# Low parts of the down weights by an accumulating transfer on GpSimd's queue, instead of VectorE's difference

## Chip, cores and metric

One core of a Trainium2 chip. The metric is the device time of one execution in microseconds. The kernel before took 1913.95 us (median of 3 runs, 1913.91 to 1914.23).

## What is computed

A decoder trunk of two layers on 512 tokens with 1024 features, all in float32. Each layer is a feed-forward block, a mixer and a second feed-forward block; the mixer is a gated linear attention (GLA) in layer 0 and a stick-breaking attention (SB) in layer 1. There are therefore four feed-forward blocks. Cut to what matters here:

```python
def swiglu(h, w_gate, w_up, w_down):
    return (jax.nn.silu(h @ w_gate) * (h @ w_up)) @ w_down

for i in range(DEPTH):
    x = x + 0.5 * swiglu(rmsnorm(x, ffn1_norm[i]), ffn1_w_gate[i], ffn1_w_up[i], ffn1_w_down[i])
    ...                                   # the mixer
    x = x + 0.5 * swiglu(rmsnorm(x, ffn2_norm[i]), ffn2_w_gate[i], ffn2_w_up[i], ffn2_w_down[i])
return rmsnorm(x, final_norm)
```

`w_gate` and `w_up` are 1024 x 2816, `w_down` is 2816 x 1024.

## The kernel before

**Numbers in two parts.** TensorE multiplies in fp32r, a shortened float32. To keep the precision, each operand v is split into a high part, v rounded to fp32r, and a low part, v minus the high part. A product is then three matmuls: high x high, low x high, high x low (`mm3`, L62 to L65). In the trace `wh` and `wl` are the high and low parts of weights; `hh` and `hl` (`nh`, `nl`, `xh`, `xl`, `th`, `tl`) are those of activations.

**The weight stream.** All weights pass through `Chunk`, `Entry` and `Feed` in the order of use. `Chunk.load` (L77) issues the load on SyncE's (SP's) queue, L85. Chunks of the down weights carry `few = True` and go to the tile `rawd`, which has two buffers of 512 KB; other chunks go to `raw`, two buffers of 1 MB. `Entry.split` (L94) makes the two parts of each unit of 128 x 1024 elements: ScalarE casts the raw unit into `wh` (L103), and VectorE subtracts, `wl = raw - wh` (L105). `wh` and `wl` have four buffers each, shared by all kinds of units. `Feed.start` splits up to two entries ahead of the one that is multiplied, and loads up to five ahead.

**The feed-forward block.** The 2816 inner features go in chunks of 256, the chunks in groups (`GROUPS`). Gate and up of a group are multiplied, and between them the down products of the group before. A down unit (`down`, L261) is 24 matmuls of 128 x 512 into the bank `ps_d`; VectorE then adds half of the bank to the residual (L276). A block has 22 down units, and the last block 18, since its last group goes through `back_tok`; that makes 84. From chunk 3 on the gate's products, and from chunk 2 on those of up, go by seven products of half size (L487, banks `ps_w`, `ps_z`, `ps_q`). VectorE then makes sums of the raw weights (tile `s`), which are split like weights. In this steady stage one gate or up chunk by seven products and one down unit take turns. ScalarE copies the first product out of `ps_w` (L522) and of `ps_q` (L530) before a second product is added to the same bank. Where a group ends, several down units follow each other, at the end of a block four or five.

**What sets the order.** The program is written in the order of the entries, and a scheduler then places the instructions of each engine's queue; each engine runs its queue in order and waits on semaphores. Transfers of one queue are issued in order. GpSimd's queue holds little: a few constants, the small gate weights of the GLA mixer (L703 to L722) and one load for the final norm (L1144).

Of the kernel before, what the change touches and what calls it, by code (L numbers as in the profile page):

```python
# [18 lines left out]
P = 128  # L19
T = 512  # L20
# [10 lines left out]
def decoder(ctx: ExitStack, tc: tile.TileContext, a: dict, out: bass.AP):  # L31
    nc = tc.nc

    # ---------------------------------------------------------------- pools
# [16 lines left out]
    # ------------------------------------------------------------ constants  # L51
# [15 lines left out]
    # --------------------------------------------------------- weight stream  # L67
    # Every weight matrix passes through here in the order of use: chunks of 1 MB are
    # loaded, cut into units of 4 KB a partition, split into high and low parts, and
    # multiplied. An entry is one or more units with the products that use them.  # L70
# [17 lines left out]
    class Entry:  # L88
        """units: (chunk, view of it, n, m); body(W) yields between parts of the products."""
# [4 lines left out]
        def split(self):  # L94
            if self.W is None:
                self.W = []
                for ch, view, n, m in self.units:
                    r = view(ch.load())
                    few = n * m < 1024
                    pool, x, bufs = (st["few"], "v", 1) if few else (wp, "w", 4)  # L100
                    h = pool.tile([P, n, m], F32R, tag=x + "h", bufs=bufs, name="wh")
                    l = pool.tile([P, n, m], F32R, tag=x + "l", bufs=bufs, name="wl")
                    st["cut"] = nc.scalar.copy(h, r).ins  # L103
                    with tc.issue_after(st["gains"]):
                        nc.vector.tensor_tensor(out=l, in0=r, in1=h.bitcast(F32), op=ALU.subtract)  # L105
                    self.W.append((h, l))
# [46 lines left out]
    def feat(ch, f, evac, tag=None, defer=None):  # L153
        """features f*128.. of a [P, KD, 256] chunk on partitions, all tokens"""

        def body(W):
            (wh, wl), = W
            ps = psum("ps_f", tag)
            for part in (range(0, KD // 2), range(KD // 2, KD)):
                for k in part:  # L160
                    mm3(ps, wh[:, k], wl[:, k], st["h"][k], st["l"][k], k == 0, k == KD - 1)
                if part[-1] == KD - 1:
                    if defer is None:
                        evac(ps)
                    else:
                        defer.append((evac, ps))
                yield

        feed.q.append(Entry([(ch, lambda t: t[:, :, f * P : (f + 1) * P], KD, P)], body))

    def tok(w, c0, evac, tag=None):
        """columns c0..c0+256 with the tokens on partitions; evac(i, ps[P, 256])"""
        ch = Chunk(cols(w, c0, 256), KD, 256)

        def body(W):
            ps = None
            for i in range(NT):
                if i % 2 == 0:
                    ps = psum("ps_t", tag)
                o = ps[:, (i % 2) * 256 : (i % 2) * 256 + 256]  # L180
                s = slice(i * P, (i + 1) * P)
                for k in range(KD):
                    wh, wl = W[k // 4]
                    mm(o, st["h"][k][:, s], wh[:, k % 4], k == 0, False)
                    mm(o, st["h"][k][:, s], wl[:, k % 4], False, False)
                    mm(o, st["l"][k][:, s], wh[:, k % 4], False, k == KD - 1)
                if i % 2:
                    evac(i - 1, ps[:, 0:256])
                    evac(i, o)
                yield  # L190

        feed.q.append(
            Entry([(ch, (lambda t, u=u: t[:, u * 4 : u * 4 + 4]), 4, 256) for u in range(2)], body)
        )

    def back(w, r0, nf, hs, scale, nxt, late=0, tags=(None,) * 8):
        """x[d] += scale * sum_f w[r0 + f, d] h[f]; nxt(k) runs when x[k] is done.
        The last `late` blocks of h come late: their products wait for the end."""
# [62 lines left out]
    def down(w, r0, nf, hs, part, nxt):  # L261
        """x[d] += 0.5 * sum_f w[r0 + f, d] h[f] for the 8 / nf blocks d of a part"""
# [22 lines left out]
    def back_tok(w, r0, nf, hs, done):  # L285
        """the same with tokens on partitions: done(dh, i, ps) gets 512 features of token tile i"""
# [23 lines left out]
    # ----------------------------------------------------------------- norms  # L310
# [24 lines left out]
    def stats_a(tag=None):  # L335
        """r4[token, tile]: 1 / rms of the residual"""
        if st["ss"] is None:
            sums = st["sums"]
        else:
            ps = psum("ps_st", tag)  # L340
            for i in range(NT):
                mm(ps[:, i : i + 1], st["ss"][:, i * P : (i + 1) * P], ones[:, 0:1], True, True)
            sums = ps[:, 0:NT]
        st["r4"] = rstd(sums, NT)
# [15 lines left out]
    def stats_b(tag=None):  # L360
        """R[any partition, token]: the same along the free axis"""
# [11 lines left out]
    def two_halves(between=None):  # L373
        """the next two entries, the first half of both before the second"""
        feed.finish()
        g = [feed.start(), feed.start()]
        for i in range(3):
            for x in g:
                next(x, None)
            if i == 0 and between is not None:  # L380
                between()
# [13 lines left out]
    def act(o, i, fn, **kw):  # L395
        """an activation of the Exp and Ln tables, queued behind their load"""
        with tc.issue_after(st["tab"]):
            st["last"] = nc.scalar.activation(o, i, fn, **kw).ins

    # ------------------------------------------------------------------- FFN  # L400
    class FFN:
        """The chunks of 256 features go in groups: gate and up, with down for the group
        before between them. From product NORMED on the input is scaled by 1/rms ahead of
        it. The gate's products from chunk SEVEN on, and those of up for the chunks SEVEN_UP,
        go by Winograd's form of Strassen's scheme: seven products of half size for the
        2 x 2 halves of features, inputs and tokens."""
# [5 lines left out]
        def __init__(self, wg, wu, wd, gi, nxt, first=False, last=False):  # L412
# [6 lines left out]
            for group, (c0, c1) in enumerate(self.GROUPS):  # L419
                slots, put = 2 * (c1 - c0), 0  # L420
                for i in range(slots):
# [5 lines left out]
                    if first and c == 0:  # L427
                        # the first products wait for no more of the weights than they need
# [16 lines left out]
                    # the sums are made of the residual as it came  # L445
# [16 lines left out]
        def seven(self, ch, group=None):  # L462
            """256 features of gate, or of up with its group. With A = [features, inputs] and B = [inputs, tokens] in
            halves and the sums S of A and T of B (see sums):
            C11 = A11 B11 + A12 B21, U = A11 B11 + S2 T2, C12 = U + S1 T1 + S4 B22,
            C21 = U + S3 T3 + A22 T4, C22 = U + S3 T3 + S1 T1"""
# [47 lines left out]
            def body_1(W):  # L514
                ax, s = W
                # a bank takes no second group of products before its first one is complete
# [41 lines left out]
        def t_half(self, i, j):  # L558
            """T(i + 1) of input block j"""
# [17 lines left out]
        def normed_input(self):  # L577
            """the scaled input, and T1 = B12 - B11, T2 = B22 - T1, T3 = B22 - B12, T4 = B21 - T2"""
# [21 lines left out]
        def sums(self):  # L600
            def piece(i):
                # in the place of the unscaled input
# [50 lines left out]
    # ------------------------------------------------------------------- GLA  # L653
    class GLA:
# [44 lines left out]
        def gate_weights(self):  # L699
            # low-rank gate: columns 0:16 take the high parts, 32:48 the low parts  # L700
# [53 lines left out]
        def levels(self, h):  # L754
            """S[s, t] = sum_k k[s] q[t] exp(b[t] - b[s]) for s <= t within 128-token chunks:
            blocks of B tokens against the B before them, each side decayed to their border"""
# [22 lines left out]
            def seconds(t, B):  # L779
                """the second block of every pair of blocks in each of the 128-token chunks"""  # L780
# [11 lines left out]
            for li in range(len(LEVELS)):  # L792
# [4 lines left out]
                # the rows up to the last first block  # L797
# [158 lines left out]
    # -------------------------------------------------------- stick-breaking  # L956
    class SB:
        # token tile i of a head lies in bank BK[i][0] at column BK[i][1]
# [50 lines left out]
        def weights_log(self, p, e):  # L1009
            """y[t, s] = log of the weight of s for t, -1e30 and less where s >= t"""  # L1010
# [3 lines left out]
            for bk, tiles in ((1, (2,)), (2, (1, 0)), (0, (3,))):  # L1014
# [6 lines left out]
                for n_, i in enumerate(tiles):  # L1021
                    # tile 0 is as wide as tile 1: no product is narrower than 256
# [50 lines left out]
        def values(self, p):  # L1073
            # the two heads of a pair fill the two halves of the array's columns
# [57 lines left out]
    # ------------------------------------------------------------ the program  # L1132
    # gain rows: ffn1 0..1, mix 2..3, ffn2 4..5 (by layer), then o_norm at column 48
# [8 lines left out]
    def to_tokens(tp):  # L1142
        fin = st["fin"] = tp.tile([P, D], F32, tag="s", bufs=4, name="fin")
        nc.gpsimd.dma_start(fin, a["final_norm"].partition_broadcast(P))  # L1144
        # in place: half of the features of all tokens at a time
# [11 lines left out]
    def last(dh, i, ps):  # L1157
        """the residual of token tile i is complete for 512 features; then the final norm"""
# [103 lines left out]
def _constants():  # L1262
    s, t = np.arange(P)[:, None], np.arange(P)[None, :]
    # for level B: the rows s against the second blocks t of every pair of blocks
# [27 lines left out]
```

## Time and profile before

| | |
|---|---|
| median of 3 runs | 1913.95 us |
| span of the profiled execution | 1913.4 us |
| TensorE busy | 1893.6 us, 99% |
| VectorE busy | 1462.7 us, 76% |
| ScalarE busy | 943.6 us, 49% |
| GpSimd busy | 6.8 us |
| moved by DMA | 179.05 MB, mean 94 GB/s |
| granted TensorE clock | 0.999 |

The profiled execution spent 1913.4 us from its first to its last instruction; that is 0.55 us less than the median of the timed runs. A busy engine is one that has an instruction in flight; an engine's idle time is put down to the instruction or transfer whose semaphore came last. In a row of the profile, "wl<-rawd,wh" is the tile written and the tiles read, by the program's names, and L105 is the line of the kernel.

### The profile page before, as it was taken

To read this page: it belongs to the slowest core of one execution; us is meant where nothing else is said; L and a number is where in the kernel's file an instruction comes from. 1 tells how busy PE (TensorE), PEld (TensorE's weight loads), DVE (VectorE), ACT (ScalarE), POOL (GpSimd) and SP (SyncE) were. 2 spreads that over 40 slices of the span, in tenths; PEclk is the share of its full clock that TensorE was granted. 3 is DMA by queue.
4 is the path that set the end of the run, shared out by engine and by line. 5 is a ranking of instruction groups with operands and counts; after the bars stand their busy time and mean duration, and the time that the engine had idled before them with its cause. 6 is when DMAs were issued, how large, how long until landed. Compare 5 with 4: busy or idle time off the path is not lost.

```text
span 1913.4 us, 28787 instructions
## 1 busy us (share of the span) xinstructions
PE 1893.6 (99%) x11789; PEld 1687.9 (88%) x11789; DVE 1462.7 (76%) x2314; ACT 943.6 (49%) x1450; POOL 6.8 (0%) x16
## 2 busy tenths in 40 slices
PE   8999999999999999999999999999999999999998
PEld 7999999889887899999989999998888788899997
DVE  7978777775666977877788778776877779777775
ACT  6534434443554544444453444445878745344444
POOL 0000000100000000000000000000000000000000
PEclk9999999999999999999999999999999999999999
DMA  5423332312123223332233333223221123333321
GB/s 156 144 89 108 103 111 90 96 46 65 60 73 110 89 89 112 105 114 78 78 113 119 100 101 108 79 89 100 66 67 59 63 89 110 99 100 105 116 78 66
DMA packets 177511, 179.05 MB, mean 94 GB/s; under 512 B 3906, under 2 KB 167924, under 8 KB 177380
## 3 DMA queue, kind: packets, MB, share of 16 engines
q1 hardware_dynamic: 176912, 176.24, 29.3%
q8 instruction: 92, 1.51, 0.3%
q0 software_dynamic: 368, 0.95, 0.2%
q14 instruction: 39, 0.32, 0.1%
q10 hardware_dynamic: 100, 0.03, 0.0%
HBM read 175.11 MB, written 2.10 MB: 93 GB/s over the span
## 4 chain that ended last, share of the span: by engine, by line
PE 96%; DVE 2%; DMA 1%; ACT 1%; issue 0%; POOL 0%; SPq 0%; DVEq 0%; POOLq 0%; ACTq 0%
PE ps_d L60 24%; PE ps_f L60 20%; PE ps_w L487 15%; PE ps_z L487 10%; PE ps_q L487 10%; PE ps_t L60 5%; PE ps_b L60 3%; PE ps_S L60 1%; PE ps_z L1019 1%; PE ps_bt L60 1%; PE ps_oT L1081 1%; PE ps_T L1066 1%; PE ps_o L60 1%; DMA x<-in_x_dram 0%; DMA raw<-in_ffn_w_up_dram 0%; DVE wl L105 0%
## 5 line engine op out<-in xcount | busy, mean ns | idle before, releaser
L105 DVE TENSOR_TENSOR wl<-raw,wh 128x1024 fp32r<-128x1024 f32 x244 | 261.4, 1072 | 94.7 <-ACT wh L103 72.8
L103 ACT CAST wh<-raw 128x1024 fp32r<-128x1024 f32 x244 | 226.0, 931 | 142.3 <-PE ps_f L60 44.5
L60 PE MATMUL ps_d<-hh,wh 128*128 128x512 f32 x672 | 262.9, 391 | 0.0
L60 PE MATMUL ps_d<-hh,wl 128*128 128x512 f32 x672 | 262.7, 391 | 0.0
L60 PE MATMUL ps_d<-hl,wh 128*128 128x512 f32 x672 | 262.3, 390 | 0.0
L103 ACT CAST wh<-s 128x1024 fp32r<-128x1024 f32 x136 | 142.7, 1049 | 153.9 <-PE ps_q L487 84.1
L276 DVE SCALAR_TENSOR_TENSOR x<-ps_d,x 128x512 f32<-128x512 f32 x184 | 126.0, 688 | 101.1 <-PE ps_d L60 100.7
L105 DVE TENSOR_TENSOR wl<-s,wh 128x1024 fp32r<-128x1024 f32 x136 | 166.4, 1223 | 32.4 <-ACT wh L103 27.4
L60 PE MATMUL ps_f<-xh,wh 128*128 128x512 f32 x448 | 182.1, 407 | 2.9 <-DVE q L682 1.5
L60 PE MATMUL ps_f<-xl,wh 128*128 128x512 f32 x448 | 175.4, 392 | 0.0
L60 PE MATMUL ps_f<-xh,wl 128*128 128x512 f32 x448 | 175.0, 391 | 0.0
L103 ACT CAST wh<-rawd 128x1024 fp32r<-128x1024 f32 x84 | 88.4, 1052 | 160.1 <-PE ps_d L60 139.2
L487 PE MATMUL ps_z<-th,wl 128*128 128x256 f32 x544 | 154.0, 283 | 0.0
L487 PE MATMUL ps_z<-th,wh 128*128 128x256 f32 x544 | 154.0, 283 | 0.0
L487 PE MATMUL ps_z<-tl,wh 128*128 128x256 f32 x544 | 153.9, 283 | 0.0
L487 PE MATMUL ps_w<-nl,wh 128*128 128x256 f32 x544 | 153.6, 282 | 0.0
L487 PE MATMUL ps_w<-nh,wl 128*128 128x256 f32 x544 | 153.4, 282 | 0.0
L487 PE MATMUL ps_w<-nh,wh 128*128 128x256 f32 x544 | 153.4, 282 | 0.0
L60 PEld LDWEIGHTS ps_d<-hl,wh 128*128 128x128 f32 x672 | 126.1, 188 | 27.6
L60 PEld LDWEIGHTS ps_d<-hh,wh 128*128 128x128 f32 x672 | 126.3, 188 | 25.5
L60 PEld LDWEIGHTS ps_d<-hh,wl 128*128 128x128 f32 x672 | 126.3, 188 | 24.9
L105 DVE TENSOR_TENSOR wl<-rawd,wh 128x1024 fp32r<-128x1024 f32 x84 | 102.9, 1225 | 46.3 <-ACT wh L103 33.4
(246 smaller groups left out, 4725.3 us busy)
## 6 DMA issues: line engine op xcount, KB each, us to landing
raw<-in_ffn_w_gate_dram SPq DMA_DIRECT2D x43, 1024.0 KB, 5.4
raw<-in_ffn_w_up_dram SPq DMA_DIRECT2D x43, 1024.0 KB, 5.3
rawd<-in_ffn_w_down_dram SPq DMA_DIRECT2D x84, 512.0 KB, 3.5
raw<-in_gla_w_in_dram SPq DMA_DIRECT2D x12, 1024.0 KB, 5.3
raw<-in_sb_w_in_dram SPq DMA_DIRECT2D x16, 512.0 KB, 3.9
raw<-in_gla_w_out_dram SPq DMA_DIRECT2D x4, 1024.0 KB, 5.0
raw<-in_sb_w_in_dram SPq DMA_DIRECT2D x4, 1024.0 KB, 5.1
raw<-in_sb_w_out_dram SPq DMA_DIRECT2D x4, 1024.0 KB, 5.1
```

Source lines behind the costliest of these rows:

```text
L60: nc.tensor.matmul(ps, l, r, start=first, stop=last)
L103: st["cut"] = nc.scalar.copy(h, r).ins
L105: nc.vector.tensor_tensor(out=l, in0=r, in1=h.bitcast(F32), op=ALU.subtract)
L276: nc.vector.scalar_tensor_tensor(out=xs[k], in0=ps, scalar=0.5, in1=xs[k], op0=ALU.mult, op1=ALU.add)
L487: nc.tensor.matmul(o, l_, r_, start=first and j + n == 0, stop=j == 3 and n == 2, skip_group_check=True)
L1019: nc.tensor.matmul(o_, l_, r_, start=first, stop=last, skip_group_check=True)
L1066: nc.tensor.transpose(ps[:, c0 : c0 + P], ys[yb][:, yc + j * P : yc + (j + 1) * P], ident)
L1081: nc.tensor.matmul(po[e * 64 : e * 64 + 64, j * P : T], self.v[j][:, c : c + 64], self.wt[p, e][bk][:, c0 : c0 + n], start=j == 0, stop=j ...
```

## The change

In `Entry.split`, for the units of down chunks alone, ScalarE writes the negated raw chunk into `wl`, rounded to fp32r like the high part, so that it holds the negated high part. Then a transfer from GpSimd's queue adds the raw chunk onto it in place: `wl = -wh + raw`. VectorE's difference stays for all other units.

```diff
                     h = pool.tile([P, n, m], F32R, tag=x + "h", bufs=bufs, name="wh")
                     l = pool.tile([P, n, m], F32R, tag=x + "l", bufs=bufs, name="wl")
                     st["cut"] = nc.scalar.copy(h, r).ins
+                    if ch.few and not few:
+
+                        nc.scalar.activation(l, r, AF.Copy, scale=-1.0)
+                        nc.gpsimd.dma_start(out=l, in_=r, accum_op=ALU.add)
+                        self.W.append((h, l))
+                        continue
                     with tc.issue_after(st["gains"]):
                         nc.vector.tensor_tensor(out=l, in0=r, in1=h.bitcast(F32), op=ALU.subtract)
                     self.W.append((h, l))
```

In the changed kernel the negated copy is L106 and the transfer L107; lines below have numbers larger by 6. TensorE's queue holds the same matmuls in the same order. The rest of the diff is comments and empty lines.

## The prediction

> **What bounds the kernel now.** I read the page's busy line and its chain of waits first, then what TensorE waited for, then one period of the steady stage and one end of a group in the timeline.
>
> ```profile
> span 1913.4 us, 28787 instructions
> PE 1893.6 (99%) x11789; PEld 1687.9 (88%) x11789; DVE 1462.7 (76%) x2314; ACT 943.6 (49%) x1450; POOL 6.8 (0%) x16
> ...
> PE 96%; DVE 2%; DMA 1%; ACT 1%; issue 0%; POOL 0%; SPq 0%; DVEq 0%; POOLq 0%; ACTq 0%
> ```
>
> TensorE is busy for 99% of the span and is 96% of the chain that ended last. VectorE, which the change relieves, is busy for 76% and carries 2% of that chain. The list of TensorE's waits says what a relief could give at most:
>
> ```profile
> PE ps_g L1210 <- DMA gl<-in_gla_o_norm_dram: 5.8, 1, 5.8
> PE ps_f L60 <- DVE q L682: 1.5, 1, 1.5
> PE ps_x L1217 <- DMA x<-in_x_dram: 1.4, 4, 0.7
> PE ps_f L60 <- DVE x L211: 1.4, 1, 1.4
> PE ps_o L60 <- DVE on L885: 0.7, 1, 0.7
> PE ps_b L60 <- ACT oh L902: 0.5, 1, 0.5
> PE ps_z L1019 <- DVE r L1052: 0.2, 1, 0.2
> PE ps_oT L1081 <- ACT wt L398: 0.2, 1, 0.2
> ```
>
> All of it is 11.7 us, and the four rows behind VectorE make 1.5 + 1.4 + 0.7 + 0.2 = 3.8 us. They stand in the mixers and in their output products (L682, L211, L885, L1052). No product of the down weights (ps_d) is among them, and none waited for L105. So the difference that the change removes is hidden in full today; the question is whether its substitute is hidden as well.
>
> **The change part by part.** These two groups are the removed work and the cast that stays beside it:
>
> ```profile
> L103 ACT CAST wh<-rawd 128x1024 fp32r<-128x1024 f32 x84 | 88.4, 1052 | 160.1 <-PE ps_d L60 139.2
> ...
> L105 DVE TENSOR_TENSOR wl<-rawd,wh 128x1024 fp32r<-128x1024 f32 x84 | 102.9, 1225 | 46.3 <-ACT wh L103 33.4
> ```
>
> *Removed from VectorE:* 84 differences of 1225 ns, 102.9 us of its 1462.7. Worth to the end: nothing, by the list of TensorE's waits.
>
> *Added to ScalarE:* 84 negated copies of one raw chunk each. No such operation is in the trace; the cast has the same input and output shape and takes 1052 ns, so 84 x 1.05 = 88 us more on an engine that is busy for 49%. The low end and the value taken are the cast's 1.05 us; the high end is the 1.22 us that the same shape takes on VectorE. ScalarE's queue in the steady stage, where one chunk of gate or up by seven products alternates with one down unit:
>
> ```order
> L502 ACTIVATE o_1599<-ps_w 128x256
> L103 CAST wh<-s_1659 128x1024
> L103 CAST wh<-s_1712 128x1024
> L508 ACTIVATE o_1599<-o_1599 128x256
> L103 CAST wh<-raw 128x512
> L508 ACTIVATE o_1668<-o_1668 128x512
> L103 CAST wh<-rawd 128x1024
> L522 COPY c_1773<-ps_w 128x256
> L530 COPY c_1801<-ps_q 128x256
> ```
>
> And the same place after the change (lines below the edit count 6 more):
>
> ```order
> L508 ACTIVATE o_1606<-ps_w 128x256
> L103 CAST wh<-s_1666 128x1024
> L103 CAST wh<-s_1719 128x1024
> L514 ACTIVATE o_1606<-o_1606 128x256
> L103 CAST wh<-raw 128x512
> L514 ACTIVATE o_1675<-o_1675 128x512
> L106 ACTIVATE wl<-rawd 128x1024
> L103 CAST wh<-rawd 128x1024
> L528 COPY c_1781<-ps_w 128x256
> L536 COPY c_1809<-ps_q 128x256
> ```
>
> The negated copy stands ahead of the cast, so the transfer can start one copy after the buffers come free; the cast and the copy of ps_w move back by one copy. One period of this stage, on ScalarE (the last row is the next period's cast), then on TensorE and its weight load:
>
> ```profile
> 186.57 1.06 ACT L103 CAST wh<-rawd 128x1024 fp32r<-128x1024 f32 x1 [1.79 <-PE ps_d L60]
> 187.96 0.37 ACT L522 COPY c<-ps_w 128x256 f32<-128x256 f32 x1 [0.33 <-PE ps_w L487]
> ...
> 190.90 0.37 ACT L530 COPY c<-ps_q 128x256 f32<-128x256 f32 x1 [2.56 <-PE ps_q L487]
> ...
> 202.11 1.06 ACT L103 CAST wh<-rawd 128x1024 fp32r<-128x1024 f32 x1 [3.59 <-PE ps_d L60]
> ```
> ```profile
> 190.64 0.28 PE L487 MATMUL ps_w<-nh,wh 128*128 128x256 f32 x1
> ...
> 196.40 0.40 PE L60 MATMUL ps_d<-hh,wh 128*128 128x512 f32 x1
> 196.63 0.40 PE L60 MATMUL ps_d<-hh,wl 128*128 128x512 f32 x1
> ```
> ```profile
> 196.40 0.19 PEld L60 LDWEIGHTS ps_d<-hh,wl 128*128 128x128 f32 x1
> ```
>
> Queued behind the new instruction is the copy of ps_w, which must be read before TensorE adds to that bank again at 190.64. It would end at 186.57 + 1.05 + 1.05 + 0.37 = 189.0 us, 1.6 us early (1.4 with the high price). The next copy starts at 190.90 behind idle time. So ScalarE's part is nothing on the path.
>
> *Added on GpSimd's queue:* 84 accumulating transfers, each of 512 KB. Call A the time from the end of the negated copy to the landing of the sum. The copy ends at 186.57 + 1.05 = 187.6; the first product with the low part runs at 196.63, and its weights are loaded from 196.40 on. So in the steady stage A may be 8.8 us before TensorE waits. The trace has no accumulating transfer; its nearest rows are these:
>
> ```profile
> raw<-in_ffn_w_gate_dram SPq DMA_DIRECT2D x43, 1024.0 KB, 5.4
> ...
> rawd<-in_ffn_w_down_dram SPq DMA_DIRECT2D x84, 512.0 KB, 3.5
> ...
> fin<-in_final_norm_dram POOLq DMA_DIRECT2D x1, 512.0 KB, 4.0
> ```
> ```profile
> DMA to landing us min/median/max: 3.2/3.5/9.4
> ```
>
> A plain transfer of 512 KB from this same queue lands in 4.0 us (fin). Another 512 KB in a transfer cost 5.4 - 3.5 = 1.9 us (gate's chunk against a down chunk). The accumulation reads the destination as well as the source. Low end: the second read costs nothing, A = 4.0. Taken: one more pass, A = 4.0 + 1.9 = 5.9, as the row of fin is nearest (same queue, size and destination shape). High end: two more passes, 7.8; and 9.4, the slowest of the 84 down loads. At 5.9 the steady stage keeps 8.8 - 5.9 = 2.9 us, and the cost is nothing.
>
> The Trainium skill gives the same order of price (Collectives: The Full Stack, "The bandwidth ceiling"): a reducing transfer runs at half the copy's rate since it reads two sources, and the addition itself is free. By that the transfer part alone doubles, which I would estimate as a landing near 5.9 too; no run here shows it yet.
>
> *Moved on SP's queue:* a raw down buffer (two of them) comes free only when the transfer has landed, 5.9 us after the copy instead of 1.2 us after the cast. In the steady stage that has room: a unit comes every 202.11 - 186.57 = 15.5 us, and there are two buffers. It is tight where down units follow each other, at the end of the feed-forward blocks. SP's queue there, before (the two GLA weight loads are the next stage's):
>
> ```order
> L85 DMA raw<-in_ffn_w_gate_dram 128x8x256
> L85 DMA rawd<-in_ffn_w_down_dram 128x4x256
> L85 DMA raw<-in_ffn_w_up_dram 128x8x256
> L85 DMA raw<-in_gla_w_in_dram 128x8x256
> L85 DMA rawd<-in_ffn_w_down_dram 128x4x256
> L85 DMA raw<-in_gla_w_in_dram 128x8x256
> L85 DMA rawd<-in_ffn_w_down_dram 128x4x256 x2
> ```
>
> and after:
>
> ```order
> L85 DMA raw<-in_ffn_w_gate_dram 128x8x256
> L85 DMA raw<-in_ffn_w_up_dram 128x8x256
> L85 DMA rawd<-in_ffn_w_down_dram 128x4x256
> L85 DMA raw<-in_gla_w_in_dram 128x8x256 x2
> L85 DMA rawd<-in_ffn_w_down_dram 128x4x256 x3
> ```
>
> The last three down loads now stand behind both GLA loads, so these don't wait for the later buffers. ScalarE's queue at the same place, before:
>
> ```order
> L530 COPY c_3457<-ps_q 128x256
> L103 CAST wh<-rawd 128x1024 x2
> L573 CAST hh<-o_3416 128x512
> L103 CAST wh<-rawd 128x1024
> L573 CAST hh<-o_3478 128x512
> L103 CAST wh<-rawd 128x1024
> ```
>
> and after:
>
> ```order
> L106 ACTIVATE wl<-rawd 128x1024
> L536 COPY c_3475<-ps_q 128x256
> L103 CAST wh<-rawd 128x1024 x2
> L106 ACTIVATE wl<-rawd 128x1024
> L579 CAST hh<-o_3434 128x512
> L579 CAST hh<-o_3497 128x512
> L103 CAST wh<-rawd 128x1024
> L106 ACTIVATE wl<-rawd 128x1024
> L103 CAST wh<-rawd 128x1024
> L106 ACTIVATE wl<-rawd 128x1024
> ```
>
> Both casts of hh, the last two blocks that this group's down products multiply, now stand behind the second of the two casts in a row and its negated copy. The place in the trace:
>
> ```profile
> 324.94 1.05 ACT L103 CAST wh<-rawd 128x1024 fp32r<-128x1024 f32 x1 [1.60 <-issue]
> ...
> 330.98 2.17 ACT L103 CAST wh<-rawd 128x1024 fp32r<-128x1024 f32 x2
> 336.12 0.62 ACT L573 CAST hh<-o 128x512 fp32r<-128x512 f32 x1 [2.98 <-DVE o L511]
> 336.93 1.05 ACT L103 CAST wh<-rawd 128x1024 fp32r<-128x1024 f32 x1 [0.18 <-DMA rawd<-in_ffn_w_down_dram]
> 338.11 0.62 ACT L573 CAST hh<-o 128x512 fp32r<-128x512 f32 x1
> 341.93 1.05 ACT L103 CAST wh<-rawd 128x1024 fp32r<-128x1024 f32 x1 [3.20 <-PE ps_d L60]
> ```
> ```profile
> 341.69 0.39 PE L60 MATMUL ps_d<-hh,wh 128*128 128x512 f32 x1
> ...
> 358.01 0.39 PE L60 MATMUL ps_d<-hh,wh 128*128 128x512 f32 x1
> 358.23 0.39 PE L60 MATMUL ps_d<-hh,wl 128*128 128x512 f32 x1
> ```
>
> Number the five casts 1 to 5. Unit 5's raw buffer is unit 3's, and unit 3's is unit 1's. So after the change: unit 1's copy ends at 326.0; + A; load 3.5; cast and copy 2.1; + A; load 3.5; cast and copy 2.1; + A = 337.2 + 3A. Its first low part is wanted at 358.0, so A may be 6.9 us there. At 5.9 there are 3.1 us to spare at the last landing. The casts of hh wait for unit 3: its load lands at 326.0 + 5.9 + 3.5 = 335.4, its cast and copy end at 337.5, so the first cast of hh ends near 338.1 and the second, wanted by the unit that starts at 341.69, near 338.7 as today; that bears an A of some 9 us. This happens at three of the four blocks (the last one ends otherwise), and a longer A costs 3 us for each us of it.
>
> *The sum:* 0 on TensorE's path. The span stays 1913.4 us, and the median of the runs is 0.55 above it: 1914.0.
>
> **The rivals.**
>
> *Slower: the sum lands too late.* The point is A = 6.9 at the ends of blocks and 8.8 in the steady stage. How many units run at the steady distance is read from what ended ScalarE's wait before the cast:
>
> ```profile
> its engine sat idle before it (us, times) until:
>   PE ps_d L60: 139.2, 47
> ```
>
> In 47 of 84 the buffer came free with the product before. So the price is 3 x 3 x (A - 6.9) + 47 x (A - 8.8): at A = 7.8, +8 us (1922); at 8.7, +16 us (1930); at 9.4, 22 + 28 = +50 us (1964). For it: no accumulating transfer is in the trace, an adder may be much slower than a copy, and these share the engines with the weight loads:
>
> ```profile
> 186.30:201.90 15.60, 15.60 (x110) 14.61 (x109) 11.16 (x16) 6.69 (x10) 0.00 (x0) 1.00 0.38 119
> ```
>
> Against it: the 16 DMA engines are busy for 0.38 of that period only. Chance 0.22 for more than +3.8 us, of it 0.12 past 1930.
>
> *No change, but later: GpSimd's issue is held up by VectorE.* Its own issues in the trace:
>
> ```profile
> 344.55 1.04 POOL L703 DMA_DIRECT2D gr<-in_gla_w_in_dram  x1 [343.24 <-DVE wl L105]
> ...
> 365.47 0.57 POOL L718 DMA_DIRECT2D lf<-in_c_lvl_dram  x1
> ```
>
> If an issue of 0.57 us ran only while VectorE is idle (11.16 of 15.60 us busy above), it would take 0.57 / 0.28 = 2.0 us, A = 5.9 + 1.4 = 7.3, and the ends of blocks give 9 x 0.4 = 4 us: 1918. Against it: the issues shown lie beside a busy VectorE and took 0.5 to 1.0 us. Chance 0.05, counted with the slower side.
>
> The Trainium skill has this rule against such transfers (SBUF — State Buffer, "Who interferes with whom"): in its two-port modes VectorE locks GpSimd's descriptor writing out. It adds that two-input operations have no such mode.
>
> *Faster: the relief reaches TensorE.* All waits behind VectorE gone would be 1913.95 - 3.8 = 1910.1. Against it: none of the four lies in a stage with down units, whose differences are all that goes. Chance 0.03.
>
> **How the numbers follow.** 0.2% is 3.8 us, about what a measurement of this kernel can tell from no change. No change 0.70 (A up to 7.3), slower 0.27 (0.22 + 0.05), faster 0.03. The predicted time is that of no change. The range goes from 1912, a part of the relief, to 1930, the price at A = 8.7; 0.12 lies above it and about 0.03 below.
>
> **What would show it.** Right: 84 rows of wl from rawd on GpSimd's queue that land within 7 us, no row of ps_d in TensorE's list of waits, a wait list near 12 us, VectorE about 103 us less busy, ScalarE about 88 us more. Wrong: ps_d behind a DMA in that list; few waits of some us would point at the ends of blocks (third and later unit), about 47 equal ones at the steady stage. A time below 1910 would say that VectorE held TensorE in a way the list of waits doesn't show.

## The result, and the profile after

The changed kernel takes 1925.50 us (median of 4 runs, 1924.31 to 1927.33) against 1914.02 us for the kernel before on the same chip (4 runs, 1913.91 to 1914.23): 11.5 us slower, ratio 1.0059 with a 95% interval of 1.0047 to 1.0071. That lies inside the predicted range, but not at its likeliest case, which was no change. The spans of the two profiled executions differ by less, 1923.3 - 1913.4 = 9.9 us. In every run of which both are known, the changed kernel's and those of the experiments, the time is 1.7 to 2.2 us above the span; the 0.55 us that the prediction added sets the span of one execution of the kernel before against the times of others.

First the page of the changed kernel, its busy line, its chain and two of its transfers:

```profile
span 1923.3 us, 29038 instructions
PE 1895.1 (99%) x11789; PEld 1687.5 (88%) x11789; DVE 1363.4 (71%) x2230; ACT 1010.6 (53%) x1534; POOL 79.1 (4%) x100
...
PE 91%; DVE 3%; DMA 3%; ACT 2%; issue 1%; SPq 0%; ACTq 0%; POOLq 0%; DVEq 0%
...
rawd<-in_ffn_w_down_dram SPq DMA_DIRECT2D x84, 512.0 KB, 4.2
wl<-rawd POOLq DMA_DIRECT2D x84, 512.0 KB, 5.0
```

VectorE has lost 1462.7 - 1363.4 = 99.3 us of work. TensorE's share of the chain that ended last has fallen from 96% to 91%; that of DMA has grown from 1% to 3%, and that of ScalarE from 1% to 2%. The list of TensorE's waits says at which product (engine and tile that waited, what ended it; us in all, times, longest):

```profile
PE ps_st L60 <- DVE ss L326: 4.8, 1, 4.8
...
PE ps_d L60 <- DMA wl<-rawd: 0.7, 1, 0.7
...
PE ps_f L60 <- DVE xl L335: 0.6, 1, 0.6
```

These three rows are new, and they lie at the ends of blocks. So does a fourth, 0.2 us for `xh` beside the `xl` of the same end. A fifth, 1.6 us for `wh` at 19.3 us, belongs to the start, which differs from execution to execution: the first `ps_f` products of the kernel before came every 0.43 us up to 18.4 us, those of the changed kernel every 0.23 us, so that it reached the next weights sooner and waited for them. Experiments 4 and 9 have the same row. The large row isn't a product of the down weights at all. `ps_st` is the product of `stats_a` that sums the squares of the residual, the first thing that a feed-forward block needs of the residual besides its input. The wait happens once, where the second feed-forward block ends and the third begins. TensorE's timeline there, before and then after (start, duration, instruction, idle time ahead of it):

```profile
963.16 0.39 PE L60 MATMUL ps_f<-xl,wh 128*128 128x512 f32 x1
963.39 0.95 PE L60 MATMUL ps_st<-ones,ss 128*128 128x1 f32 x8
964.20 0.49 PE L60 MATMUL ps_f<-xh,wh 128*128 128x512 f32 x1
964.52 0.40 PE L60 MATMUL ps_f<-xh,wl 128*128 128x512 f32 x1
964.75 0.40 PE L60 MATMUL ps_f<-xl,wh 128*128 128x512 f32 x1
```

```profile
964.65 0.39 PE L60 MATMUL ps_f<-xl,wh 128*128 128x512 f32 x1
969.86 1.87 PE L60 MATMUL ps_st<-ones,ss 128*128 128x1 f32 x8 [4.82 <-DVE ss L326]
...
972.16 0.63 PE L60 MATMUL ps_f<-xh,wl 128*128 128x512 f32 x1
972.59 0.63 PE L60 MATMUL ps_f<-xl,wh 128*128 128x512 f32 x1
```

Two losses stand side by side. From the last `ps_f` to `ps_st` it is 5.21 us where it was 0.23. And behind the gap the products start every 0.43 us (972.16, 972.59), where before it was every 0.23 (964.52, 964.75). The windows of the changed kernel show why; the clock column is the one after the engines' busy times, 1.00 being full speed:

```profile
960.00:969.58 9.58, 5.04 (x23) 3.84 (x21) 9.17 (x13) 7.25 (x11) 0.00 (x0) 1.00 0.55 172
969.58:976.41 6.83, 6.55 (x19) 5.51 (x20) 2.09 (x11) 0.35 (x2) 0.00 (x0) 0.50 0.69 219
976.41:985.00 8.59, 8.59 (x43) 7.23 (x42) 5.71 (x8) 4.74 (x6) 0.00 (x0) 1.00 0.01 3
```

TensorE came out of its wait at half clock and stayed there until 976.41 us.

Both kernels have the same 11789 matmuls in the same order, so the start times of each can be subtracted. At 20 us the changed kernel is 0.8 us ahead (the start, as said), at the end 9.75 us behind. It falls back by 1.4 us at 371 us (the end of the first feed-forward block, `xh` and `xl` late), by 1.0 us at 948 us (the one wait for a low part), by 5.0 us ahead of `ps_st`, and by 3.1 us in `ps_st` and the slow products behind it. That is 10.5 of the 10.6 us. Some 8 us are lost in one place.

**Where the lateness comes from.** The chain of waits of the changed kernel in this stretch, followed back from `ps_st` (start, us, what):

```profile
921.13 4.96 DMA wl<-rawd
926.11 5.06 DMA rawd<-in_ffn_w_down_dram
...
933.55 6.83 DMA wl<-rawd
...
940.43 5.85 DMA rawd<-in_ffn_w_down_dram
...
946.38 0.15 ACT wh L103
...
947.34 1.05 ACT wl L106
948.39 0.61 ACT xh L334
...
969.20 0.61 DVE ss L326
969.82 0.04 issue
969.86 1.87 PE ps_st L60 x8
```

It begins with unit 1's accumulating transfer. Unit 3's raw load waits until that has landed, its own transfer follows its cast and copy, and unit 5's load waits for that one. Then comes ScalarE's queue, after the change:

```profile
938.06 1.05 ACT L103 CAST wh<-rawd 128x1024 fp32r<-128x1024 f32 x1 [3.77 <-DMA rawd<-in_ffn_w_down_dram]
939.01 1.06 ACT L106 ACTIVATE wl<-rawd 128x1024 fp32r<-128x1024 f32 x1
946.38 1.05 ACT L103 CAST wh<-rawd 128x1024 fp32r<-128x1024 f32 x1 [6.32 <-DMA rawd<-in_ffn_w_down_dram]
947.34 1.05 ACT L106 ACTIVATE wl<-rawd 128x1024 fp32r<-128x1024 f32 x1
948.29 0.71 ACT L334 ACTIVATE xh<-x,gT 128x512 fp32r<-128x512 f32 x1
```

and before:

```profile
936.43 1.05 ACT L103 CAST wh<-rawd 128x1024 fp32r<-128x1024 f32 x1 [3.20 <-PE ps_d L60]
939.83 0.72 ACT L328 ACTIVATE xh<-x,gT 128x512 fp32r<-128x512 f32 x1 [2.35 <-DVE x L276]
```

Unit 5's cast comes at 946.38 instead of 936.43, and what is queued behind it is the next block's work: `xh` of the first of eight residual blocks at 948.29 instead of 939.83, 8.5 us late. VectorE's queue stands still with it, since the low part `xl` waits for `xh`, and the next residual addition stands behind `xl` (VectorE's timeline):

```profile
949.03 0.75 DVE L335 SCALAR_TENSOR_TENSOR xl<-x,gT,xh 128x512 fp32r<-128x512 f32 x1 [8.74 <-ACT xh L334]
949.70 0.68 DVE L282 SCALAR_TENSOR_TENSOR x<-ps_d,x 128x512 f32<-128x512 f32 x1
```

Eight rounds of addition, `xh`, `xl` and squares follow. Two of them take 5.75 us on VectorE (additions at 952.90, 958.65 and 964.39; before, at 945.36, 951.11 and 956.86), where TensorE makes a unit in 5.44 us. So they hardly make the time up, and the last sum `ss` is done at 969.8 instead of 962.5, 7.3 us late.

### The profile page after: what moved, and what is told of

It is laid out like the page before. It is cut to its first block, busy times and chain, and to the rows that moved or that the text cites. A ratio compares the mean times of both kernels' runs of the same rounds, so it can differ in the third digit from the quotient of the medians.

```text
span 1923.3 us, 29038 instructions
## 1 busy us (share of the span) xinstructions
PE 1895.1 (99%) x11789; PEld 1687.5 (88%) x11789; DVE 1363.4 (71%) x2230; ACT 1010.6 (53%) x1534; POOL 79.1 (4%) x100
## 4 chain that ended last, share of the span: by engine, by line
PE 91%; DVE 3%; DMA 3%; ACT 2%; issue 1%; SPq 0%; ACTq 0%; POOLq 0%; DVEq 0%
PE ps_d L60 21%; PE ps_f L60 19%; PE ps_w L493 15%; PE ps_z L493 10%; PE ps_q L493 10%; PE ps_t L60 5%; PE ps_b L60 3%; PE ps_S L60 1%; DMA wl<-rawd 1%; PE ps_z L1025 1%; PE ps_bt L60 1%; DMA rawd<-in_ffn_w_down_dram 1%; PE ps_oT L1087 1%; PE ps_T L1072 1%; DVE wl L111 1%; PE ps_o L60 1%
## 5 line engine op out<-in xcount | busy, mean ns | idle before, releaser
L106 ACT ACTIVATE wl<-rawd 128x1024 fp32r<-128x1024 f32 x84 | 89.0, 1060 | 166.9 <-PE ps_d L60 117.3
L60 PEld LDWEIGHTS ps_d<-hh,wh 128*128 128x128 f32 x672 | 126.3, 188 | 25.4
L107 POOL DMA_DIRECT2D wl<-rawd x84 | 72.4, 862 | 1778.5 <-DVE o L517 802.4
```

The source lines that it names most:

```text
L60: nc.tensor.matmul(ps, l, r, start=first, stop=last)
L106: nc.scalar.activation(l, r, AF.Copy, scale=-1.0)
L107: nc.gpsimd.dma_start(out=l, in_=r, accum_op=ALU.add)
```

## The experiments

Theory A says just this: the raw buffers at a block's end come free only when a transfer lands, and the next block's `xh` and sums stand behind unit 5's cast. The rivals were B, that ScalarE's added 89 us cost the time, and C, that the transfers slow down everything they run beside. Each run was compared with runs of the kernel before on the same chip. The diffs are against the changed kernel, but that of 2 against 1, that of 7 against 5, and that of 9 and 10 against the kernel before.

**1. The last group's units by VectorE's difference** (4 units in each of the first three blocks, 12 of 84; `acc` is a new flag of a chunk that chooses between transfer and difference).

```diff
             else:
                 for x in downs:
-                    down(*x)
+                    down(*x, acc=False)
```

> As after the change, but the four down units of the last group of the first three blocks (12 of 84) go back to VectorE's difference. Theory A (block ends: unit 5's raw load waits for unit 3's transfer, which waits for unit 1's; ScalarE's queue holds the next block's scaled residual behind unit 5's cast, so ps_st is late where block 2 meets block 3): the 5.2 us gap before ps_st goes, and the slow matmuls behind it; 1914.0 to 1915.5 us, the upper end if the 1.2 us that the changed run spends outside its span belongs to the transfers. Rival B (ScalarE's 88 us of copies delay everything a little): 72 of 84 copies stay, about 1924 us. Rival C (the 45 MB of transfers slow loads or matmuls throughout): 72 of 84 stay, about 1924 us.

Measured: 1916.20 us (1914.54 to 1917.55), ratio 1.0009 (1.0000 to 1.0018), 0.7 us above the expected range. No wait for `ps_st`. So with 72 of the 84 transfers in place most of the loss is gone. Of the rest, 0.4 us is a wait for a low part in the last block (1642 us); the larger row lies at the same block end as before:

```profile
PE ps_d L60 <- DVE hl L582: 1.0, 1, 1.0
```

There unit 3's load still waited for unit 1's transfer. VectorE stood still for 3.7 us ahead of unit 3's difference, and `o` and `hl` behind it on VectorE came late.

**2. The complement: only these 12 by transfer.**

```diff
-    def down(w, r0, nf, hs, part, nxt, acc=True):
+    def down(w, r0, nf, hs, part, nxt, acc=False):
...
-                    down(*x, acc=False)
+                    down(*x, acc=True)
```

> The opposite part: only those 12 units go by negated copy and transfer, the other 72 by VectorE's difference. Theory A: nearly the whole loss stays, 1922 to 1926 us, with a gap of 4 to 6 us before ps_st at the meeting of blocks 2 and 3. Rivals B and C: 12 of 84 of the loss, 1915 to 1916 us.

Measured: 1915.02 us (1914.44 to 1916.10), ratio 1.0003 (0.9995 to 1.0012): no loss. That misses the expectation; the last group alone isn't enough. ScalarE's timeline in this run says what was left out of the theory:

```profile
939.40 1.03 ACT L104 CAST wh<-rawd 128x1024 fp32r<-128x1024 f32 x1
940.34 0.72 ACT L336 ACTIVATE xh<-x,gT 128x512 fp32r<-128x512 f32 x1
```

Unit 1 belongs to the group before the last. With its low part made by VectorE, its buffer comes free early, the whole row of loads moves up, and unit 5's cast comes at 939.40, not 946.38. So the theory has to be A': the lateness is made by the row of transfer, load, transfer, load that begins at unit 1.

**3. All 84 by transfer, but two of the last four raw chunks (units 3 and 5) in free buffers of another pool**, so that unit 5's load waits for no transfer.

```diff
+                elif self.side:
+                    self.t = st["tp"].tile([P, self.n, self.m], F32, tag="s", bufs=4, name="raws")
...
+        ch.side = end and part % 2 == 1
```

> All 84 units by transfer, but in the last group every second raw chunk lies in a buffer of the weight sums (tile s), free by then, so that unit 5's load waits for no transfer. Theory A: ScalarE's 6.3 us wait for that load goes, no gap before ps_st, 1914 to 1916 us. Rivals B and C: copies and transfers are all there, 1924 to 1926 us.

Measured: 1914.94 us (1913.64 to 1919.85), ratio 1.0004 (0.9995 to 1.0013). The same number of transfers, copies and sums, and the 11.5 us are gone; neither `ps_st` nor `ps_d` is in its list of waits. That speaks against B and C: it is the reuse of the buffers.

**4. The copies alone:** 84 negated copies on ScalarE, no transfer, the low part by VectorE's difference as before.

```diff
                         nc.scalar.activation(l, r, AF.Copy, scale=-1.0)
-                        nc.gpsimd.dma_start(out=l, in_=r, accum_op=ALU.add)
-                        self.W.append((h, l))
-                        continue
```

> ScalarE makes all 84 negated copies, but no transfer follows; VectorE's difference overwrites them. Theory A: raw buffers come free about 2 us later than before, no load is late by more than that, 1914 to 1916 us. Rival B (ScalarE's load): 1924 to 1926 us. Rival C: 1914 us.

Measured: 1914.34 us, ratio 1.0000 (0.9991 to 1.0009). Ten executions lie between 1913.72 and 1915.22 us; an eleventh took 6648.21 us, and what held it up isn't known. B is out.

**5. Only units 1 to 5 at the end of the second feed-forward block by transfer**, 5 of 84 (`two` is true for that block).

```diff
-                        down(*downs[put])
+                        down(*downs[put], acc=two and group == 5 and put == 1)
...
             else:
                 for x in downs:
-                    down(*x)
+                    down(*x, acc=two)
```

> Only 5 of the 84 low parts go by the accumulating transfer: units 1 to 5 at the end of the second feed-forward block, the one that another feed-forward block follows at once. Theory A' (two raw buffers, so unit 3's load waits for unit 1's transfer and unit 5's load for unit 3's; the next block's scaled residual and sums of squares stand behind unit 5's cast on ScalarE, and ps_st comes late): the gap ahead of ps_st is back at about 4 to 5 us, with slow matmuls behind it, and the time is 1920 to 1924 us, most of the +11.5. Rival (the cost is spread over the 84 units, or over the three block ends alike): 5/84 to 1/3 of 11.5, so 1914.5 to 1918 us.

Measured: 1923.08 us (1921.74 to 1924.32, 5 runs), ratio 1.0044 (1.0032 to 1.0057), +8.8 us on the 1914.25 of before. The wait is back in full:

```profile
PE ps_st L60 <- DVE ss L328: 4.8, 1, 4.8
```

Five transfers out of 84 make three quarters of the loss.

**6. The complement: 79 by transfer, these five by difference.** The same edit with the flags reversed.

> The complement of the one before: 79 of 84 by the transfer, units 1 to 5 at the end of the second feed-forward block by VectorE's difference. Theory A': no gap ahead of ps_st, no slow matmuls behind it; what is left are the waits of about 1 us at the other two ends, so 1914.5 to 1917 us. Rival (spread over units or block ends): 1921 to 1925 us.

Measured: 1915.43 us (1914.84 to 1917.74), ratio 1.0007 (0.9998 to 1.0016), +1.2 us. Its list of waits has no `ps_st`, but 0.5 us for `xl` at the end of the first block and 0.4 us for `u` at 1196 us. The interval doesn't tell the 1.2 us from none. So 5 and 79 transfers nearly add up, 8.8 + 1.2 = 10.0 of the 11.5 us, and the place is settled.

**7. Only two of these five, units 1 and 3.**

```diff
-                    down(*x, acc=two)
+                    down(*x, acc=two and x[4] == 1)
```

> Only 2 of the 84 low parts go by the accumulating transfer: units 1 and 3 at the end of the second feed-forward block; all others by VectorE's difference. Theory A' (two landings and two loads in a row before unit 5's cast, and the sums behind that cast): unit 5's cast at about 944 us as with five transfers, one copy of 1.05 us less ahead of the sums, so a gap of about 4 us ahead of ps_st, slow matmuls behind it (2 to 3 us more), 1919 to 1923 us. Rival (all five must go by the transfer, or the cost lies in their low parts' own lateness): no gap, 1914 to 1916 us.

Measured: 1914.49 us (1914.26 to 1916.93), ratio 1.0002 (0.9994 to 1.0011). My expectation was wrong: I had taken it that unit 5 always gets unit 3's buffer. SyncE's queue, VectorE and ScalarE in this run:

```profile
925.19 9.83 SPq L86 DMA_DIRECT2D rawd<-in_ffn_w_down_dram  x3
```
```profile
933.41 1.22 DVE L112 TENSOR_TENSOR wl<-rawd,wh 128x1024 fp32r<-128x1024 f32 x1
```
```profile
938.41 1.05 ACT L104 CAST wh<-rawd 128x1024 fp32r<-128x1024 f32 x1 [4.77 <-DMA rawd<-in_ffn_w_down_dram]
```

The last of the three loads is issued at 925.19 + 9.83 - 0.37 = 934.65, just as unit 4's difference ends (934.63) and before unit 3's transfer, issued at 931.96, can have landed 4.8 us later. Unit 5 took the buffer of unit 4. So both buffers must be held by transfers for the row to form; one difference among them is a way out. `xh` came at 941.35, and `ps_st` waited for 0.7 us. TensorE was 1.3 us ahead of the kernel before here (a product at 929.43 that came at 930.72 before), so `xh` was 941.35 + 1.3 - 939.83 = 2.8 us late: about 2 us of lateness are covered, each further us is lost. The changed kernel agrees: its TensorE was 0.5 us behind, `xh` 948.29 - 0.5 - 939.83 = 8.0 us late, and 1.0 + 5.0 = 6.0 us were lost; so does experiment 5, where TensorE was 1.3 us ahead, `xh` 946.00 + 1.3 - 939.83 = 7.5 us late, and 0.4 + 5.0 = 5.4 us were lost.

**8. A plain transfer in place of the sum,** all 84; the low parts then hold the raw weights.

```diff
-                        nc.gpsimd.dma_start(out=l, in_=r, accum_op=ALU.add)
+                        nc.gpsimd.dma_start(out=l.bitcast(F32), in_=r)
```

> The price of the adder: the change with all 84 transfers, but each a plain copy of the raw chunk into wl instead of a sum onto it, so that the low parts hold the raw weights and the output isn't the reference's. If the addition costs what the row of fin suggests (a plain 512 KB from this queue 4.0 us, the sum 5.0), a transfer lands in about 4.0 us, unit 5's load comes 2 us earlier, and the gap ahead of ps_st is about 3 us instead of 5.2: 1920 to 1923 us. If the landing is that of any transfer here, added or not: 5.0 us, the same gap, 1924 to 1927 us.

Measured: 1914.99 us (1914.15 to 1916.08), ratio 1.0002 (0.9993 to 1.0011), less than both expectations. The group of these transfers in this run, and unit 5's cast:

```profile
L107 POOL DMA_DIRECT2D wl<-rawd x84: 527/528/667, 81.4 to 1863.8; - x84
...
DMA to landing us min/median/max: 2.8/2.9/5.5
```
```profile
939.46 1.05 ACT L103 CAST wh<-rawd 128x1024 fp32r<-128x1024 f32 x1 [2.75 <-DMA rawd<-in_ffn_w_down_dram]
```

A plain 512 KB within the chip lands in 2.9 us, not in the 4.0 of the row of fin (which comes from DRAM), and the sum in 5.0: the addition costs 2.1 us and issues of 0.86 us instead of 0.53. Without it unit 5's cast comes at 939.46 and `xh` at 941.38, which is 1.8 us late with TensorE 0.2 us ahead, within the 2 us that are covered. So the loss hangs on the price of the addition.

**9 and 10. Lateness without any transfer:** the kernel before, with the last square of the second feed-forward block held back by 4 and by 8 copies on the idle GpSimd.

```diff
             nc.scalar.activation(sq, xs[k], AF.Square)
+            for _ in range(wait):
+                nc.gpsimd.tensor_copy(sq, sq)
```

> No transfer at all: the kernel before, with the last sums of squares of the second feed-forward block held back by 4 copies of 128x512 in place on GpSimd (about 3 to 4 us, against some 1 us that ps_st has to spare). Theory A' says that lateness of these sums alone makes the cost: a gap of 2 to 3 us ahead of ps_st. If TensorE is also slow behind a gap of that length, the time grows by more than the gap (up to +6); if not, by the gap alone: 1916 to 1918. Rival (the sums have room, it was the transfers that cost): 1914 to 1914.5.

> The same with 8 copies (6 to 8 us): a gap of 5 to 7 us ahead of ps_st, without any transfer. Theory A' with the slow matmuls as a consequence of the gap: the matmuls behind it come at about 0.43 us instead of 0.23 for some 3.5 us, and the time is the gap + 3: 1922 to 1925 us. If the slow matmuls came from the transfers or something else of the change: the gap alone, 1919 to 1921.

Measured: 1915.61 us (1914.84 to 1916.85), ratio 1.0007 (0.9998 to 1.0016), with 4; 1917.82 us (1917.01 to 1919.15), ratio 1.0018 (1.0009 to 1.0027), with 8. Both lie below what was expected. The gaps were smaller, 0.9 and 1.5 us of waiting, since the scheduler moved `ps_st` back by 2 and by 11 products. But the slow products came with the longer one (TensorE's timeline with 8 copies):

```profile
966.41 1.05 PE L60 MATMUL ps_st<-ones,ss 128*128 128x1 f32 x8 [1.54 <-DVE ss L322]
...
967.66 0.63 PE L60 MATMUL ps_f<-xh,wh 128*128 128x512 f32 x1
968.09 0.63 PE L60 MATMUL ps_f<-xh,wl 128*128 128x512 f32 x1
...
971.05 0.39 PE L60 MATMUL ps_f<-xl,wh 128*128 128x512 f32 x1
```

Eight products of 0.43 instead of 0.23 us cost 1.6 us, and 1.5 + 1.6 = 3.1 of the measured 3.6. Behind the shorter gap there were none. So lateness of these sums is enough to make both losses, and the half clock can follow a pause of TensorE without any accumulating transfer.

## Why the prediction was only half right, point by point

- **VectorE's 102.9 us are worth nothing: right.** The four rows of the list before that it could have shortened are there still, 1.5, 1.2, 0.6 and 0.4 us against 1.5, 1.4, 0.7 and 0.2.
- **ScalarE's copies cost nothing: right.** A copy took 1.06 us (1.05 taken), and experiment 4 shows them free. ScalarE's busy time grew by 1010.6 - 943.6 = 67.0 us, not by the 88 expected; in part because neighbours overlap (a cast at 938.06 takes 1.05 us, the copy behind it starts at 939.01).
- **The steady stage keeps room: right.** The sum lands in 5.0 us in the middle (4.5 to 8.2), with 0.3 us from the copy's end to its issue, against the 5.9 taken and the limit of 8.8, and none of those units waited. The Trainium skill's rule that a reducing transfer runs at half the copy's rate (Collectives: The Full Stack, "The bandwidth ceiling") comes near: an estimate by it, twice the 2.9 us of the plain transfer, is 5.8, where 5.0 was measured.
- **GpSimd's issue held up by VectorE: not so.** An issue took 0.86 us (0.85 to 1.00), not 2.0, beside a VectorE that is 71% busy. No run here showed the lockout of which the Trainium skill speaks (SBUF — State Buffer, "Who interferes with whom").
- **The end of a block: this is the step that failed.** The prediction had the row of buffers right (unit 1's transfer, unit 3's load, its transfer, unit 5's load), but it asked only when the low parts and the casts of `hh` would be late. There it was nearly right: one wait for a low part, 0.7 us in all 84 (its own sign of being wrong, `ps_d` behind a DMA, but a small one). What stands behind unit 5's cast on ScalarE's in-order queue, the next block's `xh` and squares, was never followed to the product that wants them, although ScalarE's queue was quoted to just before that point. The "0 on TensorE's path" for the blocks' ends was therefore no result of the sum but a gap in it. The runs showed 8.1 us at one such end, 5.0 of waiting and 3.1 of slow products. That the time still lies inside the range is luck: its upper part was the price of low parts landing late, at an A of 8.7 us.
- **Its terms were also too small there.** By the prediction's 5.9 and 3.5 us, unit 5's load would land 5.9 + 3.5 + 2.1 + 5.9 + 3.5 = 20.9 us after unit 1's copy; it took 946.3 - 920.9 = 25.4. Each load is released by the landing of one transfer just as the next transfer starts, so they run together. The last pair, both issued at 940.4, in the changed kernel, first the transfer, then the load:

```profile
DMA to landing us min/median/max: 8.2/8.2/8.2
```
```profile
DMA to landing us min/median/max: 5.9/5.9/5.9
```

  The medians are 5.0 (all 84 sums) and 3.5 (the 84 loads before). Even with the predicted 20.9, `xh` would have come at 941.8 + 1.9 for cast and copy = 943.7, 3.4 us late by the same count, and some 1.4 us would have been lost.
- **"This happens at three of the four blocks" at 3 us for each us of A: wrong in kind.** One end in three pays, the one that a feed-forward block follows at once (experiments 5 and 6); at the first end 1.4 us went, at the third nothing. And past the 2 us that are covered the price is not the lateness alone, but the half clock behind it, 3.1 us, which was in no term.

## What to carry to other kernels

When a change makes a buffer come free later, follow the buffer to the load that wants it, that load to the instruction that waits for it, and then read on down that engine's queue: what stands behind is late too, and may belong to the next stage. A kernel whose TensorE is 99% busy in the mean is judged at its seams, where several units follow each other and transfer, load and transfer run in a row. A pause of TensorE should be priced with the slow products that may follow it.

## What the runs showed of the hardware

- The half clock. In the changed kernel it lasted from 969.58 to 976.41, 6.83 us (shown above). In experiment 5, behind a wait of the same length, and in experiment 10 it was (clock column as above):

```profile
965.34:972.17 6.83, 4.61 (x15) 4.03 (x16) 4.04 (x13) 2.28 (x4) 0.00 (x0) 0.50 1.00 317
```
```profile
967.60:971.01 3.41, 3.41 (x9) 2.63 (x8) 1.74 (x5) 2.53 (x3) 0.00 (x0) 0.50 0.00 0
```

  So it came in stretches of 3.41 us, one or two of them. It began 0.28 us before TensorE resumed (changed kernel), 2.22 us before (experiment 5, 967.56), and 1.19 us after (experiment 10, 966.41); so the same wait left 6.55 us of half clock to the products in the one and 4.61 in the other. The Trainium skill (TensorE: Matmul & The Clock Gate, "What's actually happening") speaks of a free-running window of about 3.4 us that decides on half or full clock; the 3.41 us agree. The Trainium skill (TensorE: Matmul & The Clock Gate, "Why this matters for your kernels") asks for no gaps over some 3 us; here 1.54 us were enough once, while longer waits at another place had no effect, 1.67 us in experiment 9 and 1.89 us in experiment 8 (TensorE's timeline there):

```profile
611.80 0.50 PE L60 MATMUL ps_f<-xh,wh 128*128 128x512 f32 x1 [1.89 <-DVE x L217]
612.13 0.39 PE L60 MATMUL ps_f<-xh,wl 128*128 128x512 f32 x1
612.37 0.39 PE L60 MATMUL ps_f<-xl,wh 128*128 128x512 f32 x1
```

  So the length of the wait alone doesn't decide. Whether its place in such a window does, or the small products of `ps_st` behind it, these runs leave open.
- A transfer of 512 KB within the chip lands in 2.9 us, one that adds in 5.0 (8.2 beside a load), with an issue of 0.86 us on GpSimd instead of 0.53.
- The 84 sums moved 44 MB on GpSimd's queue. Where they stayed clear of each other's buffers (experiment 3), they slowed nothing that TensorE waited for.
